# One transpose for the sample's values in the mLSTM layer, written into the keys' PSUM bank

## The chip, the cores and the metric

One core of a Trainium2 chip runs the whole step. Its engines work side by side: TensorE (PE) multiplies and transposes and writes to PSUM, VectorE (DVE) and ScalarE (ACT) read PSUM and do the elementwise work, GpSimd (POOL) does small masks and copies, SyncE (SP) issues the transfers. The metric is the device time of one execution in microseconds; each number is the median of several runs.

## What is computed

The reference is one step of a two-layer trunk over 256 prompt tokens and 64 sample tokens (8 sequences of 8 tokens), 320 in all. Layer 0 mixes with a spatial gate, layer 1 with an mLSTM matrix memory; a gated convolution network follows each. The change lies in layer 1. Cut to what matters there:

```python
p = x @ w_in
qk, new_buf = causal_dwconv(qk_pre, conv_buf, conv_w, conv_b)
k = qk[..., QK_B // 2:].reshape(bsz, s, H_B, DK_B) * (DK_B ** -0.5)
v32 = v.astype(jnp.float32).reshape(bsz, s, H_B, DV_B)
sc = jnp.einsum('bhtd,bhsd->bhts', qc, kc) * w_intra
num = w_inter[..., None] * jnp.einsum('bhtd,bhde->bhte', qc, C) \
    + jnp.einsum('bhts,bhse->bhte', sc, vc)
kg = kc * g[..., None]
C_new = decay[..., None, None] * C + jnp.einsum('bhsd,bhse->bhde', kg, vc)
```

There are 8 heads; keys have 128 elements a head, values 256. Products run in float32 split into a high part (fp32r) and a low part, with three products for one.

## The kernel before

Activations lie with features on the partitions and the 320 tokens on the free axis. Every projection is a row of blocks of 128 output features: `block` (with `chunk` and `take`) multiplies one 128-column slice of the weights by all tokens into one PSUM bank of the pool `psm` (three banks, tag `pm`). The pool `psa` (five banks, tag `pa`) holds the rest. `take` also runs the pipeline of the weights: `prefetch` issues the transfer four pieces ahead (line 127) and, one piece ahead, splits a landed piece into its high part `wh` on ACT (line 154) and its low part `wl` on DVE (line 155).

All PE instructions are pinned to the order in which the program writes them (`mm`, `tr`, `pin`; lines 54 and 57). The instructions of the other engines are ordered by a planner among those that are ready; `tc.issue_after(x)` adds that what its body writes on the engine of x is issued behind x.

Layer 1 (`layer_b`) loops over the heads `h`. One turn, in PE's order: the q block and its convolution (`qk_epi`), the k block, the state products and numerators of the head before (`inter`, `numer`), the first v block (`v_epi(h, 0)`), `state_prompt` and the first half of `state_sample` of the head before, the second v block (`v_epi(h, 1)`), `scores`, the two blocks of the output gate (`o_epi`) with more of `state_sample`, `finish` of the head before, then `k_nat(h)`, `v_nat(h)`, and the first state products `inter(h, 0)`. From head 4 on blocks of the output projection (`early`) come between.

- `v_epi` (line 786) copies a value block from PSUM to `vT` with ACT: 320 columns (line 788), and the 64 sample columns once more (line 789), so that the third group of 128 columns holds the sample's tokens twice.
- `k_nat` (line 863) transposes the keys in three groups of 128 tokens into columns 0 to 383 of one bank, `pk`. ACT and DVE then read it in pairs: twice a pair for the sample's gated keys `kgs` (lines 878 and 879), and one pair for each of the two prompt groups, `kgh` and `kgl` (lines 886 and 887).
- `v_nat` (line 841) transposes the values: three groups of tokens by two halves of 128 features, six transposes into two banks `pv`. ACT scales each group of 256 columns into `vh` (line 851), DVE takes the low part (line 854). For the sample the rows 0 to 63 of `vh[:, 2]` hold the high part and the rows 64 to 127 the low part; this is why its tokens are there twice. ACT copies them into `vb` (lines 856 and 857).
- `vh`, `vl` and `vb` are read by `numer` and the state updates of this head, which run in the next turn of the loop.
- `split` (line 311) keeps its two instructions in `self.parts`; after `qk_epi(h, 1)` `self.parts[1]` is the DVE instruction that makes `khl`, the low part of the keys that `scores` reads.

Of the kernel before, what the change touches and what calls it, by code (L numbers as in the profile page):

```python
# [10 lines left out]
F32 = mybir.dt.float32  # L11
F32R = mybir.dt.float32r
AF = mybir.ActivationFunctionType
ALU = mybir.AluOpType
MULT, ADD, SUB, MAX = ALU.mult, ALU.add, ALU.subtract, ALU.max

P = 128
EPS = 1e-6
TP = 256
NB, NS = 8, 8  # L20
T = TP + NB * NS
# [6 lines left out]
DV = 256  # L28
# [9 lines left out]
class Net:  # L38
# [597 lines left out]
    def layer_b(self):  # L636
        nc, tc, I, O = self.nc, self.tc, self.I, self.O
# [4 lines left out]
        with ExitStack() as ctx:  # L642
            lp = ctx.enter_context(tc.tile_pool(name="lb", bufs=1))
# [109 lines left out]
            S = [dict() for _ in range(NH)]  # L753
# [31 lines left out]

            def v_epi(h, j, ps):
                vT = lp.tile([P, 384], F32, tag="vT", name="vTb", bufs=2)
                nc.scalar.copy(vT[:, :T], ps[:, :T])
                nc.scalar.copy(vT[:, T:384], ps[:, TP:T])
                S[h].setdefault("vT", []).append(vT)  # L790

            def rows_in(h):
                mb = hp.tile([P, 392], F32, tag="Mb", name="Mb", bufs=2)
                nc.sync.dma_start(mb, I["rows"][h:h + 1, :].to_broadcast([P, 392]))
                S[h]["rows"] = mb
# [44 lines left out]

            def v_nat(h):
                s = S[h]
                pv = [self.psa.tile([P, 512], F32, tag="pa", name="pv") for _ in range(2)]
                dsts = [pv[t // 2][:, (t % 2) * DV:] for t in range(3)]
                for t in range(3):
                    for e in range(2):
                        self.tr(dsts[t][:, e * P:(e + 1) * P], s["vT"][e][:, t * P:(t + 1) * P], self.ident)
                for t in range(3):
                    dst = dsts[t]
                    sc = self.rc[:, t:t + 1]  # L850
                    nc.scalar.activation(vh[:, t, :DV], dst[:, :DV], AF.Copy, scale=sc)

                    r, out = (slice(0, P), vl[:, t, :DV]) if t < 2 else (slice(64, P), vh[64:, t, :DV])
                    nc.vector.scalar_tensor_tensor(out, dst[r, :DV], sc[r], vh[r, t, :DV].bitcast(F32), op0=MULT, op1=SUB)

                nc.scalar.copy(vb[:, :DV], vh[:, 2, :DV])
                nc.scalar.copy(vb[:32, :DV], vh[32:64, 2, :DV])
# [5 lines left out]
            def k_nat(h):  # L863
                s = S[h]
                ks = s["k"][0]
                pool, tag = (self.psm, "pm") if 0 < h < NH - 1 else (self.psa, "pa")
                pk = pool.tile([P, 512], F32, tag=tag, name="pk")
                for t in range(3):
                    self.tr(pk[:, t * P:(t + 1) * P], ks[:, t * P:(t + 1) * P], self.ident)
                kgh = hp.tile([P, 2, P], F32R, tag="kgh", name="kgh", bufs=1)  # L870
                kgl = hp.tile([P, 2, P], F32R, tag="kgl", name="kgl", bufs=1)
                kgs = hp.tile([P, 2, P], F32R, tag="kgs", name="kgs", bufs=1)
                kgz = hp.tile([P, NB, P], F32R, tag="kgz", name="kgz", bufs=1)
                g = colsT[:, 2, 32 + h:33 + h]
                src = pk[:, 2 * P:3 * P]

                for i, (r, o) in enumerate(((slice(0, 32), slice(32, 64)), (slice(32, 64), slice(0, 32)))):
                    nc.scalar.activation(kgs[:, i, :], src, AF.Copy, scale=g)
                    nc.vector.scalar_tensor_tensor(kgs[o, i, :], src[r], g[r], kgs[r, i, :].bitcast(F32), op0=MULT, op1=SUB)
                s["kg"] = (kgh, kgl, kgs, kgz)  # L880
                if h < NH - 1:
                    k_mask(h)
                for t in range(2):
                    g = colsT[:, t, 32 + h:33 + h]
                    src = pk[:, t * P:(t + 1) * P]
                    nc.scalar.activation(kgh[:, t, :], src, AF.Copy, scale=g)
                    nc.vector.scalar_tensor_tensor(kgl[:, t, :], src, g, kgh[:, t, :].bitcast(F32), op0=MULT, op1=SUB)

            def k_mask(h):
                _, _, kgs, kgz = S[h]["kg"]  # L890
                if h == NH - 1:
                    for b in range(NB):
                        nc.scalar.activation(kgz[:, b, :], kgs[:, b // 4, :].bitcast(F32), AF.Copy, scale=mk[:, b:b + 1])
                    return
                for i in (0, 4):
                    nc.gpsimd.tensor_tensor(kgz[:, i:i + 4, :], kgs[:, i // 4, :].bitcast(F32).unsqueeze(1).to_broadcast([P, 4, P]),
                                            mk[:, i:i + 4].unsqueeze(2).to_broadcast([P, 4, P]), op=MULT)
# [135 lines left out]
            def early(h, r):  # L1033
                for m in self.EARLY_OUT.get((h, r), ()):
                    self.residual(m, self.block(8, lambda k: Y[k]))
# [5 lines left out]
            vh = hp.tile([P, 3, CW], F32R, name="vh")  # L1041
            vl = hp.tile([P, 2, CW], F32R, name="vl")
# [18 lines left out]
            def blk():  # L1061
                return self.block(KD, self.x_rhs)
# [3 lines left out]
            def states(h, made):  # L1066

                state_in(h)
                with tc.issue_after(made.ins):
                    for i in (0, 1):  # L1070
                        state_split(h, i)
# [10 lines left out]
            for h in range(NH):  # L1082
                if h:
                    rows_in(h)
                    qk_epi(h, 0, blk())
                    early(h, 0)
                    if h == 1:
                        inter(0, 0)
                        state_split(0, 3)
                    inter(h - 1, 1)  # L1090
                    qk_epi(h, 1, blk())
                    for i in (2, 3):
                        inter(h - 1, i)
                    numer(h - 1)
                    early(h, 1)
                    ps = blk()
                    with self.behind_split():
                        stats(h - 1)
                    v_epi(h, 0, ps)
                    state_prompt(h - 1)  # L1100
                    made = state_sample(h - 1, 0)
                    early(h, 2)
                    v_epi(h, 1, blk())
                last = h == NH - 1
                if last:
                    with tc.issue_after(made.ins):
                        made = normed(h - 1)
                    states(h, made)
                if h:
                    made = state_sample(h - 1, 1)  # L1110
                    if not last:
                        with tc.issue_after(made.ins):
                            normed(h - 1)
                scores(h)
                early(h, 3)
                if h and not last:
                    o_epi(h, 0, blk())
                if last:
                    finish(h - 1)
                    begin(0)  # L1120
                if h:
                    for i in (2, 3) if last else (2,):
                        state_sample(h - 1, i)
                if last:
                    begin(1)

                    self.prefetch(0, self.used + 2)
                early(h, 4)
                if h and not last:
                    states(h, made)  # L1130
                if h and not last:
                    o_epi(h, 1, blk())
                if h and not last:
                    finish(h - 1)
                    state_sample(h - 1, 3)
                k_nat(h)
                v_nat(h)
                if h:
                    inter(h, 0)
                    for i in (2, 3):  # L1140
                        low = state_split(h, i)
                else:
                    with tc.issue_after(self.parts[0].ins), tc.issue_after(self.parts[1].ins):
                        state_split(0, 2)
                early(h, 5)
            nc.sync.dma_start(O["b_state"], nst)

            h = NH - 1
# [8 lines left out]
            ps = blk()  # L1157
# [14 lines left out]
            for m in range(KD):  # L1172
                ps = part.get(m)
                if ps is None:
                    ps = self.block(8, lambda k: Y[8 + k])
# [154 lines left out]
```

## Time and profile before

| what | value |
|---|---|
| median of 3 runs | 953.92 us (953.64 to 953.95) |
| the profiled execution | 954.62 us |
| its span, first to last instruction | 952.9 us |
| layer 1, heads 0 to 7 (from the first k transposes of head 0 to those of head 7) | 447.6 to 671.9 us |
| mean granted TensorE clock | 0.999 |
| HBM traffic | 163 GB/s over the span |

A line of the timeline gives the start in us, the time in us, the engine, the source line, the operation, the tile written and the tiles read, the shape, and how many were merged. A line of the groups ends in the count, then the busy us and the mean ns of one, then the idle us of the engine ahead of them with what ended it. A line of the waits gives the us in total, how often, and the longest. A line of the stretches gives the bounds and the length, the busy us of each engine with its instructions, the granted clock, the share of the DMA engines and their GB/s. The chain gives the start, the us and the work on it. Matmuls are pipelined: one lasts longer than the distance to the next, so lengths on PE are read from the chain.

### The profile page before, as it was taken

What the parts mean: (1) busy time and instruction counts of PE and PEld (TensorE: products, weight loads), DVE (VectorE), ACT (ScalarE), POOL (GpSimd) and SP (SyncE); (2) the same over time, 40 slices, a digit from 0 to 9 for tenths busy, and PEclk for the clock granted to TensorE, in tenths of its full rate; (3) what the DMA queues carried; (4) which work ended last, traced back from release to release, by engine and by line L of the source; (5) the groups of instructions that cost most, each with busy time, mean ns of one, the idle gap of its engine ahead of it and who ended that gap; (6) DMA issues with size and microseconds to landing.
All of it is one profiled execution on the core that took longest, in us unless ns stands there. A gap on an engine that the chain in (4) does not pass through costs nothing.

```text
span 952.9 us, 17084 instructions
## 1 busy us (share of the span) xinstructions
PE 945.6 (99%) x6420; PEld 932.8 (98%) x6420; DVE 695.6 (73%) x1324; ACT 530.5 (56%) x978; POOL 117.6 (12%) x291
## 2 busy tenths in 40 slices
PE   9999999999999999999999999999999999999997
PEld 8889999999999999999999999999999999999997
DVE  6766976577777764559999998788888777775443
ACT  7557543454554443348877767666765544554342
POOL 3200000010000000014442312303001000000000
PEclk9999999999999999999999999999999999999999
DMA  8643346544444455565465756654474444445541
GB/s 272 209 153 133 130 134 190 175 140 150 153 156 147 141 159 156 146 215 176 155 201 185 219 174 207 198 183 133 132 250 144 156 148 145 151 150 152 145 138 56
DMA packets 55238, 156.15 MB, mean 164 GB/s; under 512 B 7492, under 2 KB 13132, under 8 KB 55156
## 3 DMA queue, kind: packets, MB, share of 16 engines
q1 hardware_dynamic: 55156, 155.06, 51.2%
q8 instruction: 51, 0.84, 0.3%
q14 instruction: 31, 0.25, 0.1%
HBM read 143.05 MB, written 11.99 MB: 163 GB/s over the span
## 4 chain that ended last, share of the span: by engine, by line
PE 93%; DVE 3%; ACT 1%; issue 1%; POOL 0%; DMA 0%; SPq 0%; POOLq 0%; ACTq 0%
PE pm L54 80%; PE pv_a L54 6%; PE num L54 2%; PE pmix L54 1%; PE pcs L54 1%; PE pCp L54 1%; PE phn L57 0%; PE psc L54 0%; DVE wl L155 0%; PE pv L57 0%; PE pc L54 0%; ACT wh L154 0%; PE pg L54 0%; DVE Cl L911 0%; DMA raw<-in_a_wv 0%
## 5 line engine op out<-in xcount | busy, mean ns | idle before, releaser
L154 ACT CAST wh<-raw 128x1024 fp32r<-128x1024 f32 (+3 forms) x256 | 256.7, 1004 | 270.8 <-PE pm L54 141.5
L155 DVE TENSOR_TENSOR wl<-raw,wh 128x1024 fp32r<-128x1024 f32 (+3 forms) x256 | 298.8, 1168 | 121.0 <-ACT wh L154 116.5
L54 PE MATMUL pm<-xh,wh 128*128 128x320 f32 x1216 | 372.2, 311 | 0.0
L54 PE MATMUL pm<-xl,wh 128*128 128x320 f32 x1216 | 370.3, 309 | 0.0
L54 PE MATMUL pm<-xh,wl 128*128 128x320 f32 x1216 | 321.2, 309 | 0.0
L54 PEld LDWEIGHTS pm<-xl,wh 128*128 128x128 f32 x1216 | 228.4, 188 | 0.2
L54 PEld LDWEIGHTS pm<-xh,wh 128*128 128x128 f32 x1216 | 228.3, 188 | 0.2
L54 PEld LDWEIGHTS pm<-xh,wl 128*128 128x128 f32 x1216 | 214.5, 188 | 0.0
L54 PE MATMUL pm<-yh_f,wh 128*128 128x320 f32 x352 | 108.8, 309 | 0.0
L54 PE MATMUL pm<-yl_f,wh 128*128 128x320 f32 x352 | 108.8, 309 | 0.0
L54 PE MATMUL pm<-yh_f,wl 128*128 128x320 f32 x352 | 108.8, 309 | 0.0
L54 PEld LDWEIGHTS pm<-yh_f,wh 128*128 128x128 f32 x352 | 66.1, 188 | 0.0
L54 PEld LDWEIGHTS pm<-yl_f,wh 128*128 128x128 f32 x352 | 66.1, 188 | 0.0
L54 PEld LDWEIGHTS pm<-yh_f,wl 128*128 128x128 f32 x352 | 66.1, 188 | 0.0
L532 DVE SCALAR_TENSOR_TENSOR fcv<-fpad,vecs,fcv 128x336 f32<-128x336 f32 x88 | 49.5, 565 | 2.1 <-ACT fcv L530 0.6
L54 PE MATMUL pm<-yh_a,wh 128*128 128x320 f32 x128 | 39.6, 310 | 0.0
L54 PE MATMUL pm<-yh_a,wl 128*128 128x320 f32 x128 | 39.5, 309 | 0.0
L54 PE MATMUL pm<-yl_a,wh 128*128 128x320 f32 x128 | 39.5, 309 | 0.0
L534 ACT ACTIVATE fgl<-fcv 128x256 f32<-128x256 f32 x44 | 18.3, 415 | 37.9 <-DVE fcv L532 37.8
L54 PE MATMUL pm<-yhb,wh 128*128 128x320 f32 x128 | 38.2, 311 | 0.0
L54 PE MATMUL pm<-ylb,wh 128*128 128x320 f32 x128 | 37.9, 309 | 0.0
L304 DVE TENSOR_TENSOR xT<-pm,xT 128x320 f32<-128x320 f32 x39 | 19.0, 488 | 24.7 <-PE pm L54 24.5
(289 smaller groups left out, 1366.5 us busy)
## 6 DMA issues: line engine op xcount, KB each, us to landing
raw<-in_f_up SPq DMA_DIRECT2D x88, 512.0 KB, 3.3
raw<-in_b_win SPq DMA_DIRECT2D x48, 512.0 KB, 4.1
raw<-in_f_dn SPq DMA_DIRECT2D x32, 448.0 KB, 3.4
C<-in_C SPq DMA_DIRECT2D x32, 258.0 KB, 3.9
out_Cs<-C SPq DMA_DIRECT2D x32, 258.0 KB, 4.0
raw<-in_a_win SPq DMA_DIRECT2D x16, 512.0 KB, 3.2
raw<-in_a_wo SPq DMA_DIRECT2D x16, 512.0 KB, 4.0
raw<-in_f_dn SPq DMA_DIRECT2D x16, 512.0 KB, 3.6
```

The costliest lines, as they stand in the source:

```text
L54: self.pin(self.nc.tensor.matmul(out, lhsT, rhs, start=start, stop=stop, skip_group_check=skip))
L154: self.last_split = self.hold(nc.scalar.copy(wh[:, :kn, :], raw[:, :kn, :]))
L155: self.last_low = nc.vector.tensor_tensor(wl[:, :kn, :], raw[:, :kn, :], wh[:, :kn, :].bitcast(F32), op=SUB)
L304: self.nc.vector.tensor_tensor(x, ps[:, :T], x, op=ADD)
L532: nc.vector.scalar_tensor_tensor(cv, pd[:, i:i + NC], self.vec(w + i * KF), cv, op0=MULT, op1=ADD)
L534: nc.scalar.activation(gl[:, :TP], cv[:, :TP], AF.Gelu_apprx_tanh)
```

## The change

For the heads 1 to 7 the sample's 64 columns of both value blocks are copied side by side into one tile `vS` instead of twice behind each other in `vT`. One transpose of `vS` then gives both halves of the features, the first in the rows 0 to 63 and the second in the rows 64 to 127. It is written to columns 384 to 511 of the bank `pk`, the columns that the keys leave free, and `pv` is one bank instead of two. ACT and DVE take the high and the low part from there in two pairs of 64 rows by 128 columns. Head 0 stays as it was.

Besides, the second value block of heads 1 to 7 runs within `tc.issue_after(self.parts[1].ins)`: the DVE instructions that it issues, which is the low part of the next piece of weights (the output gate's first block, in the last head a piece of the output projection), are issued behind `khl`.

```diff
             def v_epi(h, j, ps):
                 vT = lp.tile([P, 384], F32, tag="vT", name="vTb", bufs=2)
-                nc.scalar.copy(vT[:, :T], ps[:, :T])
-                nc.scalar.copy(vT[:, T:384], ps[:, TP:T])
+                if h:
+                    nc.scalar.copy(vT[:, :TP], ps[:, :TP])
+
+                    if not j:
+                        S[h]["vS"] = lp.tile([P, P], F32, tag="vS", name="vS", bufs=1)
+                    nc.scalar.copy(S[h]["vS"][:, 64 * j:64 * j + 64], ps[:, TP:T])
+                else:
+                    nc.scalar.copy(vT[:, :T], ps[:, :T])
+                    nc.scalar.copy(vT[:, T:384], ps[:, TP:T])
...
             def v_nat(h):
                 s = S[h]
-                pv = [self.psa.tile([P, 512], F32, tag="pa", name="pv") for _ in range(2)]
-                dsts = [pv[t // 2][:, (t % 2) * DV:] for t in range(3)]
-                for t in range(3):
+                both = "vS" in s
+                pv = [self.psa.tile([P, 512], F32, tag="pa", name="pv") for _ in range(1 if both else 2)]
+                dsts = [pv[0][:, t * DV:(t + 1) * DV] for t in range(2)] + [s["pk"][:, 384:] if both else pv[1]]
+                for t in range(2 if both else 3):
                     for e in range(2):
                         self.tr(dsts[t][:, e * P:(e + 1) * P], s["vT"][e][:, t * P:(t + 1) * P], self.ident)
-                for t in range(3):
-                    dst = dsts[t]
+                if both:
+                    self.tr(dsts[2][:, :P], s["vS"], self.ident)
+                for t in range(2):
                     sc = self.rc[:, t:t + 1]
-                    nc.scalar.activation(vh[:, t, :DV], dst[:, :DV], AF.Copy, scale=sc)
-
-                    r, out = (slice(0, P), vl[:, t, :DV]) if t < 2 else (slice(64, P), vh[64:, t, :DV])
-                    nc.vector.scalar_tensor_tensor(out, dst[r, :DV], sc[r], vh[r, t, :DV].bitcast(F32), op0=MULT, op1=SUB)
+                    nc.scalar.activation(vh[:, t, :DV], dsts[t][:, :DV], AF.Copy, scale=sc)
+                    nc.vector.scalar_tensor_tensor(vl[:, t, :DV], dsts[t][:, :DV], sc, vh[:, t, :DV].bitcast(F32), op0=MULT, op1=SUB)
+
+                lo = slice(64, P)
+                if both:
+                    for e, r in enumerate((slice(0, 64), lo)):
+                        c, sc = slice(e * P, (e + 1) * P), self.rc[r, 2:3]
+                        nc.scalar.activation(vh[:64, 2, c], dsts[2][r, :P], AF.Copy, scale=sc)
+                        nc.vector.scalar_tensor_tensor(vh[lo, 2, c], dsts[2][r, :P], sc, vh[:64, 2, c].bitcast(F32), op0=MULT, op1=SUB)
+                else:
+                    sc = self.rc[:, 2:3]
+                    nc.scalar.activation(vh[:, 2, :DV], dsts[2][:, :DV], AF.Copy, scale=sc)
+                    nc.vector.scalar_tensor_tensor(vh[lo, 2, :DV], dsts[2][lo, :DV], sc[lo], vh[lo, 2, :DV].bitcast(F32), op0=MULT, op1=SUB)
...
                 for t in range(3):
                     self.tr(pk[:, t * P:(t + 1) * P], ks[:, t * P:(t + 1) * P], self.ident)
+                s["pk"] = pk
                 kgh = hp.tile([P, 2, P], F32R, tag="kgh", name="kgh", bufs=1)
...
                     early(h, 2)
-                    v_epi(h, 1, blk())
+
+                    with tc.issue_after(self.parts[1].ins):
+                        ps = blk()
+                    v_epi(h, 1, ps)
```

## The prediction

> **What bounds the kernel now.** I read the page first, then the waits of TensorE (PE), then the chain of waits and the timeline of one head.
>
> ```profile
> span 952.9 us, 17084 instructions
> ...
> PE 945.6 (99%) x6420; PEld 932.8 (98%) x6420; DVE 695.6 (73%) x1324; ACT 530.5 (56%) x978; POOL 117.6 (12%) x291
> ...
> PE 93%; DVE 3%; ACT 1%; issue 1%; POOL 0%; DMA 0%; SPq 0%; POOLq 0%; ACTq 0%
> ```
>
> PE is busy for 945.6 of 952.9 us, and 93% of the chain that ended last is PE. Busy time alone could hide waiting, so the waits of PE over the whole span come next; this is all of them.
>
> ```profile
> PE pw L54 <- PEq L1310: 0.8, 1, 0.8
> PE num L54 <- DVE y_b L1027: 0.3, 1, 0.3
> PE pv_a L54 <- DVE wh L146: 0.2, 1, 0.2
> ```
>
> In the memory layer PE waits once, for 0.3 us. So anything taken off PE's stream is a gain to the end, anything that VectorE (DVE) or ScalarE (ACT) does besides is free as long as PE finds its data, and **a new wait of PE is lost in full**: no slack of PE is there to take it up. The chain in time order prices the stretch that the change touches, here in head 2:
>
> ```profile
> 505.60 0.33 PE pk L57 x3
> 505.93 0.66 PE pv L57 x6
> 506.58 0.47 PE num L54 x4
> 507.06 3.52 PE pm L54 x24
> ```
>
> Three key transposes (pk), six value transposes (pv), the first part of the state products (num), and then the next head's q block (pm), without a gap.
>
> **The change, part by part.**
>
> *One transpose less.* Six transposes take 0.66 us on the chain, so one is 0.11 us. Heads 1 to 7 lose one each: 7 x 0.11 = 0.77 us off PE.
>
> *The engines around it.* Rows by form of the heads 1 to 6:
>
> ```profile
> L788 ACT COPY vTb<-pm 128x320 f32<-128x320 f32 x12 | 5.0, 413 | 0.7 <-PE pm L54 0.6
> ...
> L851 ACT ACTIVATE vh<-pv,rc 128x256 fp32r<-128x256 f32 x18 | 7.8, 470 | 0.9 <-DVE vl L854 0.2
> L854 DVE SCALAR_TENSOR_TENSOR vh<-pv,rc,vh 64x256 fp32r<-64x256 f32 x6 | 2.9, 491 | 0.2
> L886 ACT ACTIVATE kgh<-pk,cols 128x128 fp32r<-128x128 f32 x12 | 4.4, 368 | 0.0
> L887 DVE SCALAR_TENSOR_TENSOR kgl<-pk,cols,kgh 128x128 fp32r<-128x128 f32 x12 | 4.1, 341 | 0.0
> ```
>
> The copy of 320 columns (413 ns) shrinks to 256; two of them per head save between nothing and 0.08 us each (a fifth of the row). The sample's ACT scaling of 256 columns (470 ns) becomes two of 64x128; the nearest row, 128x128 from the same kind of bank, is 368 ns, so 0.74 us, 0.27 more. The DVE subtraction (491 ns) becomes two at 341 ns, 0.19 more. Together under 0.5 us a head on engines for which PE does not wait; what hides it is the q and k blocks of the next head (3.52 us each), which run before the products with vh. With that cover gone it would be 7 x 0.46 = 3.2 us. I cost it at nothing.
>
> *The low parts of the output gate's weights.* The added order is that this DVE instruction (wl) issues behind the low part of the keys (khl).
>
> ```profile
> 494.06 0.27 DVE L312 TENSOR_TENSOR khl<-qs,kh 128x128 fp32r<-128x128 f32 x1
> ...
> 496.80 1.22 DVE L155 TENSOR_TENSOR wl<-raw,wh 128x1024 fp32r<-128x1024 f32 x1
> ```
>
> The gate's low part (496.80 in head 2) already comes 2.5 us behind the end of khl. The edge only fixes what happens; should the order turn without it, a wl in front would delay the keys by its 1.2 us. Cost: nothing.
>
> *Where the new transpose writes.* This decides the sum. The transpose goes to columns 384 to 511 of pk, a bank whose columns 0 to 383 ACT and DVE read eight times in `k_nat` (two kgs pairs, the kgh/kgl pairs), and `k_nat` is written ahead of `v_nat`. Does an access to one bank wait for another engine's earlier access to other columns of it? The timeline of head 2 answers it for ACT and DVE:
>
> ```profile
> 505.76 0.82 PE L57 MATMUL pv<-ident,vTb 128*128 128x128 f32 x6
> ...
> 506.20 0.35 ACT L878 ACTIVATE kgs<-pk,cols 128x128 fp32r<-128x128 f32 x1
> ...
> 506.41 1.18 DVE L1030 SCALAR_TENSOR_TENSOR ylb<-y_b,gnh,yhb 128x320 fp32r<-128x320 f32 x2
> ...
> 507.62 0.62 ACT L910 CAST Ch<-C 128x516 fp32r<-128x516 f32 x1
> ...
> 508.02 0.34 DVE L879 SCALAR_TENSOR_TENSOR kgs<-pk,cols,kgs 32x128 fp32r<-32x128 f32 x1
> ...
> 508.39 0.37 ACT L878 ACTIVATE kgs<-pk,cols 128x128 fp32r<-128x128 f32 x1
> ...
> 508.90 0.34 DVE L879 SCALAR_TENSOR_TENSOR kgs<-pk,cols,kgs 32x128 fp32r<-32x128 f32 x1
> ...
> 509.28 0.37 ACT L886 ACTIVATE kgh<-pk,cols 128x128 fp32r<-128x128 f32 x1
> ...
> 509.28 0.49 DVE L854 SCALAR_TENSOR_TENSOR vh<-pv,rc,vh 64x256 fp32r<-64x256 f32 x1
> ...
> 510.20 0.34 DVE L887 SCALAR_TENSOR_TENSOR kgl<-pk,cols,kgh 128x128 fp32r<-128x128 f32 x1
> ...
> 510.58 0.37 ACT L886 ACTIVATE kgh<-pk,cols 128x128 fp32r<-128x128 f32 x1
> ...
> 511.06 0.42 DVE L762 TENSOR_TENSOR bpad<-pm,rb 128x256 f32<-128x256 f32 x1
> ...
> 511.40 0.34 DVE L887 SCALAR_TENSOR_TENSOR kgl<-pk,cols,kgh 128x128 fp32r<-128x128 f32 x1
> ```
>
> The eight readers strictly alternate ACT, DVE, ACT, DVE in program order, though ACT's second to fourth reading needs nothing that DVE makes: at 507.62 ACT takes a state cast from further down the program instead of the second kgs, which starts only when DVE's first reading has ended. In two heads ACT even sat idle for it; the view of that ACT line has, under the idle times before it, the releaser, the us and the times:
>
> ```profile
>   DVE kgs L879: 0.3, 2
> ```
>
> So one bank is shared in program order, whatever the columns. If that holds for ACT against DVE, I take it to hold for PE's write against both, and the new transpose, fifth of the value transposes, must wait for the second kgl. Queued behind it on PE are the state products and the next head's q block, that is everything.
>
> The Trainium skill speaks against this change too: "PSUM — Partial Sum Buffer", section "PSUM bank collisions raise a hardware error", says that two engines on one bank and 32-partition quadrant collide even at disjoint columns, and that software must keep them apart by bank. By it PE has to be held back; the trace has no PE write behind a reader of the same bank, so only the ACT/DVE half of the rule is seen here.
>
> *The length of the wait.* PE's fifth value transpose would start at 505.76 + 4 x 0.11 = 506.20; the second kgl ends at 511.40 + 0.34 = 511.74: 5.5 us. The first and the last of the seven heads:
>
> ```profile
> 476.92 0.82 PE L57 MATMUL pv<-ident,vTb 128*128 128x128 f32 x6
> ...
> 483.89 0.34 DVE L887 SCALAR_TENSOR_TENSOR kgl<-pk,cols,kgh 128x128 fp32r<-128x128 f32 x1
> ...
> 672.09 0.82 PE L57 MATMUL pv<-ident,vTb 128*128 128x128 f32 x6
> ...
> 676.04 1.22 DVE L155 TENSOR_TENSOR wl<-raw,wh 128x1024 fp32r<-128x1024 f32 x1
> 677.17 0.34 DVE L887 SCALAR_TENSOR_TENSOR kgl<-pk,cols,kgh 128x128 fp32r<-128x128 f32 x1
> ```
>
> 477.36 to 484.23 is 6.9 us, 672.53 to 677.51 is 5.0; heads 3 to 6 look like head 2. Sum: 6.9 + 5 x 5.5 + 5.0 = 39 us. Upper end: add a low part of 1.2 us in front of the last kgl (as at 676.04) in the six other heads, 46. Lower end, the eight readings back to back: 4 x 0.36 + 4 x 0.34 = 2.8 us from 506.20, seven times 20. In between: the sample's subtraction at 509.28 now comes after the wait and bpad at 511.06 needs PE, so 0.9 us leave the stretch, while a low part may fill it. I take 37 us, near the order that is seen, since ylb (506.41) stays in front.
>
> *The clock after a wait.* The trace shows one long idle time of PE, at the end, and a cold start:
>
> ```profile
> 5.29 0.57 PE L54 MATMUL pv_a<-wl,xh 128*128 128x256 f32 x2
> ...
> 6.42 0.40 PE L54 MATMUL pv_a<-wl,xh 128*128 128x256 f32 x2
> ...
> 947.00:948.00 1.00, 0.01 (x1) 0.00 (x0) 0.80 (x2) 0.77 (x2) 0.00 (x0) 1.00 0.39 129
> ...
> 951.00:952.90 1.90, 0.00 (x0) 0.00 (x0) 0.00 (x0) 0.00 (x0) 0.00 (x0) 0.54 0.21 80
> ```
>
> The granted clock (third figure from the end) averages 0.54 over the last 1.9 us, so it went to half at about 951.15, 4.1 us after PE's last work; and at the start PE works some 5 us (from 0.8 to 5.8) before a pair of the same products falls from 0.57 to 0.40 us. A stall of over 4 us can therefore cost up to 5 us at half speed, 2.5 us. Between 0 and 7 x 2.5 = 17.5 us; the stalls are a little longer than that idle time, and I take a third, 6 us.
>
> "TensorE: Matmul & The Clock Gate" in the Trainium skill ("What's actually happening") lets the clock fall after one idle window of about 3.4 us that runs freely; by that roughly half of stalls of 5.3 us would meet it, about 9 us by the 2.5 above, and the trace's 4.1 us agrees with it.
>
> **Sum.** Span 952.9 + 37 + 6 - 0.8 = 995.1, with the 1.7 us around the span (954.62 profiled) 996.8; the profiled execution lies 0.7 above the median of 953.92, so **996 us**, 4.4% slower.
>
> **The rivals.** (1) *No wait, not slower.* Only overlapping columns order PE against the readers. Then 953.92 - 0.77 = 953.1, and with the 0.3 us wait gone 952.8. For it: write and reads share no column, and no PE write behind a reader is seen. Against it: ACT's readings share no column with DVE's later ones either, and wait. It decides if PE's fifth value transpose starts within about 0.1 us of the fourth. (2) *A short wait.* The planner draws the eight readings together, 20 us in all and no clock loss: 953.1 + 20 = 973. Against it: ylb, C and the split of the next weights are ready earlier and go first now. (3) *The clock falls at every stall*: 953.1 + 37 + 17.5 = 1008. For it: 4.1 us are below most stalls; against it: an idle time shorter by a microsecond may just miss it.
>
> **How the numbers follow.** The forecast 59%, no wait 14%, short wait 12%, clock each time 15%. A measurement of this kernel tells about 0.2%, 1.9 us, from no change. No wait gives -0.8 to -1.1 us, mostly inside that: same 12%, faster 2%; the other cases are slower, 86%. The range 970 to 1013 takes in the short wait and the clock, with the longest order of readings up to 46, and leaves out the case without a wait.
>
> **What would show it.** Right: in heads 1 to 7 PE idle ahead of a pv/pk transpose, released by DVE kgl, 4 to 6 us each; PE's idle time over 35 us; a granted clock below 1 in those stretches. Wrong: no such wait and some 953 us. If the wait is there but 2 to 3 us long, the readings were drawn together; if it is there and the clock stays at 1.00, the term of 6 us falls.

## The result and the profile after

The changed kernel takes 1005.9 us (median of four runs, 1003.51 to 1007.52), beside 953.93 us before: 1.054 times as long, 95% interval 1.052 to 1.056. The profiled execution took 1004.64 us with a span of 1001.8, so 48.9 us of span were added. The page after, its head, the clock in slices and the chain by engine:

```profile
span 1001.8 us, 17107 instructions
...
PE 957.5 (96%) x6413; PEld 943.1 (94%) x6413; DVE 701.6 (70%) x1331; ACT 533.4 (53%) x985; POOL 113.5 (11%) x291
...
PEclk9999999999999999999889889998999999999999
...
PE 91%; DVE 5%; ACT 2%; issue 1%; DMA 0%; POOL 0%; SPq 0%; POOLq 0%; ACTq 0%
```

PE has seven instructions fewer (6413 for 6420) and yet is busy 12 us longer, since some of its work runs slower: the clock row dips to 8 in the middle. And PE is no longer busy throughout. All the waits of PE, in total us, times and the longest:

```profile
PE pk L57 <- DVE kgl L906: 37.9, 7, 7.1
PE pw L54 <- PEq L1332: 0.8, 1, 0.8
PE pv_a L54 <- ACT wh L154: 0.2, 1, 0.2
```

Seven waits, one per changed head, all of the new transpose for the last reading of the keys' bank: 37.9 us. The releaser is an instruction of DVE, so this is an order between instructions; what the chip would do without that order, no run shows. The wait of 0.3 us for y_b that the memory layer had before is gone. The first and the last of the seven in the timeline of PE, with the idle time and its releaser in brackets; the five between are 5.5 us each:

```profile
484.69 0.47 PE L57 MATMUL pk<-ident,vS 128*128 128x128 f32 x1 [7.11 <-DVE kgl L906]
...
722.53 0.33 PE L57 MATMUL pk<-ident,vS 128*128 128x128 f32 x1 [3.37 <-DVE kgl L906]
```

The chain of waits shows what PE waits for, here in head 2 (start, us, work), which before ran from pk to pm without a gap:

```profile
515.51 0.55 DVE ylb L1049
516.07 0.40 DVE C L1026
...
516.86 0.48 DVE vl L861
517.38 0.34 DVE kgs L898
517.75 1.37 DVE wl L155
519.15 0.36 DVE kgl L906
519.54 0.38 ACT kgh L905
519.94 0.36 DVE kgl L906
520.35 0.47 PE pk L57
520.82 0.86 PE num L54 x4
521.68 5.56 PE pm L54 x24
527.24 0.47 PE num L54 x4
527.71 3.52 PE pm L54 x24
```

The eight readings of the bank still go one behind the other, with a split of the next weights' low part (wl, 1.37 us) between them, and only then does PE transpose. Behind the wait the first block of 24 products takes 5.56 us; the second takes 3.52 as always. That is the clock. The stretches in which the granted clock was 0.50 (bounds, length, busy us by engine, clock, DMA share, GB/s), and as the last row the wait of head 7:

```profile
481.70:488.50 6.80, 3.81 (x16) 3.81 (x17) 4.22 (x8) 3.02 (x8) 2.66 (x2) 0.50 0.65 196
519.30:526.00 6.70, 5.66 (x22) 5.66 (x23) 2.34 (x6) 3.17 (x9) 1.82 (x5) 0.50 0.53 140
553.40:560.20 6.80, 3.36 (x14) 3.37 (x15) 3.82 (x8) 3.50 (x10) 4.08 (x6) 0.50 0.72 223
590.90:597.70 6.80, 5.42 (x22) 5.42 (x23) 2.65 (x7) 3.34 (x9) 2.12 (x5) 0.50 0.51 146
638.70:642.10 3.40, 2.89 (x12) 2.90 (x13) 1.45 (x4) 2.24 (x7) 1.24 (x5) 0.50 0.79 240
683.10:689.90 6.80, 4.89 (x20) 4.90 (x21) 3.17 (x7) 3.34 (x9) 2.64 (x5) 0.50 0.50 98
718.50:722.60 4.10, 0.73 (x7) 0.49 (x6) 2.82 (x8) 4.06 (x14) 0.00 (x0) 1.00 0.52 161
```

Six of the seven waits cost the clock. PE worked 3.81 + 5.66 + 3.36 + 5.42 + 2.89 + 4.89 = 26.0 us within those stretches, and half of it, 13.0 us, would not have been needed at the full clock. The bill of the span: 37.9 of waits, less 0.8 for the transposes, less the 0.3 us wait that is gone, leaves 48.9 - 36.8 = 12.1 us for the clock, close to those 13. How much the clock takes differs between executions: the four ran at mean granted clocks of 0.982, 0.981, 0.975 and 0.976 and took 1003.51, 1004.64, 1007.16 and 1007.52 us, so the bill is that of one of the two milder ones.

### The profile page after: what moved, and what is told of

It reads as the page before. It is cut to its first block, busy times and chain, and to the rows that moved or that the text cites. A ratio compares the mean times of both kernels' runs of the same rounds, so it can differ in the third digit from the quotient of the medians.

```text
span 1001.8 us, 17107 instructions
## 1 busy us (share of the span) xinstructions
PE 957.5 (96%) x6413; PEld 943.1 (94%) x6413; DVE 701.6 (70%) x1331; ACT 533.4 (53%) x985; POOL 113.5 (11%) x291
## 4 chain that ended last, share of the span: by engine, by line
PE 91%; DVE 5%; ACT 2%; issue 1%; DMA 0%; POOL 0%; SPq 0%; POOLq 0%; ACTq 0%
PE pm L54 78%; PE pv_a L54 6%; PE num L54 3%; DVE wl L155 1%; PE pmix L54 1%; PE pcs L54 1%; PE pCp L54 1%; ACT yhb L1048 1%; PE psc L54 1%; DVE kgl L906 1%; DVE kgs L898 0%; DMA raw<-in_a_wv 0%; DVE vl L861 0%; PE pk L57 0%; PE pc L54 0%
## 5 line engine op out<-in xcount | busy, mean ns | idle before, releaser
L54 PEld LDWEIGHTS pm<-xh,wh 128*128 128x128 f32 x1216 | 231.1, 190 | 0.2
L54 PEld LDWEIGHTS pm<-xl,wh 128*128 128x128 f32 x1216 | 230.9, 190 | 0.2
L54 PE MATMUL pm<-yhb,wh 128*128 128x320 f32 x128 | 41.4, 334 | 0.0
L54 PE MATMUL pm<-ylb,wh 128*128 128x320 f32 x128 | 41.0, 331 | 0.0
L57 PE MATMUL pk<-ident,vS 128*128 128x128 f32 x7 | 3.2, 454 | 37.9 <-DVE kgl L906 37.9
```

Source lines behind the costliest of these rows:

```text
L54: self.pin(self.nc.tensor.matmul(out, lhsT, rhs, start=start, stop=stop, skip_group_check=skip))
L57: self.pin(self.nc.tensor.transpose(out, in_, ident))
```

## The experiments

The theory after the result: the loss is the order of the new transpose behind the eight readings of its bank, plus the clock that follows the waits. The rivals: the new tile and pairs are late, the issue order holds something back, or the bank itself is dear to share.

**A bank of its own, and the order of issue by itself.** Three kernels. The first is the change with a second value bank:

```diff
-                pv = [self.psa.tile([P, 512], F32, tag="pa", name="pv") for _ in range(1 if both else 2)]
-                dsts = [pv[0][:, t * DV:(t + 1) * DV] for t in range(2)] + [s["pk"][:, 384:] if both else pv[1]]
+                pv = [self.psa.tile([P, 512], F32, tag="pa", name="pv") for _ in range(2)]
+                dsts = [pv[0][:, t * DV:(t + 1) * DV] for t in range(2)] + [pv[1]]
```

> The change with one thing undone: the single transpose of the sample's values goes to a second pv bank of its own instead of the keys' bank. If PE waits because the write comes behind eight readings of the same bank, the wait of PE for kgl is gone and the time is the one before less seven transposes, 953.9 - 0.8 = 953.1 us (952 to 954). If the new tile vS, the two pairs of 64 rows or the added issue order were what is late, PE still waits and the time stays above 990 us.

The second is the change without the issue order; the third is the kernel before with this diff turned round, the order alone.

```diff
-                    with tc.issue_after(self.parts[1].ins):
-                        ps = blk()
-                    v_epi(h, 1, ps)
+                    v_epi(h, 1, blk())
```

> The change without its second part: the issue order of the gate's low parts behind the keys' low part is taken out. If that order costs nothing, 1006 us (1002 to 1009) with the same seven waits for kgl. If it is what holds PE or DVE back, or what keeps a 1.2 us low part out of the keys' way, the time differs by some 8 us (7 x 1.2) in either direction.

> The kernel before with the second part alone. The order is already the one of the trace before, so 953.9 us (953.3 to 954.5), no difference. If the added order holds back the low part behind khl where PE needs it, some us more.

Own bank: 956.98 us, 1.0031 of before (1.0020 to 1.0041). Its waits of PE:

```profile
PE num L54 <- DVE y_b L1046: 1.1, 2, 0.6
PE pw L54 <- PEq L1332: 0.8, 1, 0.8
PE pcs L54 <- issue: 0.6, 1, 0.6
```

No wait for kgl: with the transpose, the tile vS, the pairs and the issue order all in place, taking the write out of the keys' bank removes 49 of the 52 us. The bank that the write goes to is the cause. (Each PSUM tile here has a bank to itself, so no run separates "the same bank" from "the same tile". In heads 1 to 6 `pk` is one of the three banks of `psm`, which the projections share; that these lack a bank is not the loss, since the list after the change has no wait of a `pm`.) But 953.1 was a miss: the time is 3 us above before, not 0.8 below. Without the issue order the change takes 1005.51 us (1003.61 to 1006.45) with 37.6 us of waits for kgl, the same as with it; and the order alone gives 1.0003 of before (0.9995 to 1.0012). So the second part of the change explains nothing of the loss.

**The transpose ahead of the readings.** Same bank, same columns, another place in the program:

```diff
                 s["pk"] = pk
+                if "vS" in s:
+                    self.tr(pk[:, 384:], s["vS"], self.ident)
...
-                if both:
-                    self.tr(dsts[2][:, :P], s["vS"], self.ident)
```

> The change with the single transpose moved: it goes to the same columns of the keys' bank, but stands directly behind the three key transposes, ahead of the eight readings. If only the order behind the readings costs, 953.1 us (952 to 954) and no wait of PE for kgl. If sharing the bank itself is dear (the pairs of the sample now run behind eight readings of the keys), PE waits elsewhere or the time stays some us above 954.

965.53 us, 1.0122 of before (1.0108 to 1.0136). No wait for kgl, as the theory had it, but the rival is right as well: PE waits elsewhere. The row of its waits, and the end of the longest but one of them, in head 2, from the last reading of the keys on:

```profile
PE num L54 <- DVE vh L866: 9.1, 4, 3.6
```

```profile
513.64 0.34 DVE L906 SCALAR_TENSOR_TENSOR kgl<-pk,cols,kgh 128x128 fp32r<-128x128 f32 x1
...
516.29 0.80 ACT L818 ACTIVATE w<-Mb,cols 128x256 f32<-128x256 f32 x2 [3.26 <-DMA Mb<-rows]
517.00 0.35 ACT L865 ACTIVATE vh<-pk,rc 64x128 fp32r<-64x128 f32 x1
...
517.38 0.34 DVE L866 SCALAR_TENSOR_TENSOR vh<-pk,rc,vh 64x128 fp32r<-64x128 f32 x1 [1.81 <-ACT vh L865]
...
518.05 1.03 ACT L154 CAST wh<-raw 128x1024 fp32r<-128x1024 f32 x1
...
519.11 0.36 ACT L865 ACTIVATE vh<-pk,rc 64x128 fp32r<-64x128 f32 x1
519.50 0.36 DVE L866 SCALAR_TENSOR_TENSOR vh<-pk,rc,vh 64x128 fp32r<-64x128 f32 x1
...
519.92 0.39 PE L54 MATMUL num<-vh,Ps 128*128 128x258 f32 x1 [3.24 <-DVE vh L866]
```

The sample's two pairs now come behind the eight readings of the keys in the same bank, and the numerator product, due some 10 us behind the transposes, finds vh unfinished. The queue in the bank is not the whole of this delay: the readings end at 513.98, but ACT stands idle until 516.29 for another instruction, whose input Mb a transfer brings, takes the first pair at 517.00, and then slips a weight split of 1.03 us between the two. With the pairs at the same place in the program and a bank of their own, no wait for vh is left. So a shared bank has two prices in these kernels: the writer waits for earlier readers, and later readers wait for earlier readers and then for whatever their engine has taken up meanwhile. Of the 11.6 us, 9.1 are these waits; the longest, 3.6 us in head 7, also cost the clock for 3.4 us.

**The pairs ahead of the readings, and the own bank without the order.** To see whether anything is left of the 0.8 us, the transpose stays in the keys' bank behind the key transposes, and the two pairs are written ahead of `kgs` in `k_nat`:

```diff
+                if "vS" in s:
+                    self.tr(pk[:, 384:], s["vS"], self.ident)
+                    lo = slice(64, P)
+                    for e, r in enumerate((slice(0, 64), lo)):
+                        c, sc = slice(e * P, (e + 1) * P), self.rc[r, 2:3]
+                        nc.scalar.activation(vh[:64, 2, c], pk[r, 384:], AF.Copy, scale=sc)
+                        nc.vector.scalar_tensor_tensor(vh[lo, 2, c], pk[r, 384:], sc, vh[:64, 2, c].bitcast(F32), op0=MULT, op1=SUB)
                 kgh = hp.tile([P, 2, P], F32R, tag="kgh", name="kgh", bufs=1)
```

> The transpose behind the three key transposes in the keys' bank, and the sample's two pairs ahead of the eight readings of the keys, with the added issue order. If the 9.1 us of waits for vh, with the transpose first, come from the pairs queueing behind those readings, they are gone: 953 to 955 us. If the later keys then make PE wait for kgl, kgh or kgz, some us more.

> The same without the added issue order. If the order is what brings small waits into the kernels that have it, 953.1 us, 1 to 3 us below the one with it; if it does nothing, the same time.

> The single transpose in a bank of its own, without the added issue order. If the 0.3% by which the own bank with the order is slower than before comes from the order (a low part in front of the output gate's product and so of y_b, for which PE waits twice), 953.1 us (952.5 to 954). If it comes from the new pairs and the copies into vS, 957 us again.

| kernel | us | ratio to before, 95% | PE's waits in the memory layer |
|---|---|---|---|
| own bank, with the order | 956.98 | 1.0031 (1.0020 to 1.0041) | y_b 1.1, issue 0.6 |
| own bank, without it | 954.78 | 1.0008 (0.9999 to 1.0017) | y_b 1.1 |
| pairs first, with the order | 957.62 | 1.0038 (1.0025 to 1.0051) | vh 2.7, xT 0.8, wh 0.5 |
| pairs first, without it | 955.76 | 1.0013 (1.0004 to 1.0022) | bns 1.0, xT 0.7 |

With the pairs first the 9.1 us of waits for vh are 2.7 us for vh at another product, or none. The order costs about 2 us in both pairs of kernels; which instruction pays is not settled, since the spans of the two own-bank profiles (954.1 and 953.9) hardly differ: the one with the order is of the fastest of its seven executions, 955.78 us. None of the three reaches the 953 us that was expected, and no version is faster than before. The row of the own bank without the order says where the 0.8 us can have gone:

```profile
PE num L54 <- DVE y_b L1046: 1.1, 3, 0.4
```

The state products behind the transposes wait three times for y_b, 1.1 us, where it was once and 0.3 before. That the earlier arrival of PE only lengthens this wait is one reading of the rows and not shown. Against it stands the kernel with the order alone: it has all its transposes, its time is that of before, and its trace shows 0.9 us of waits for y_b. Where the 0.8 us went stays open.

**The clock.** PE is given work during its waits, into a bank that nobody reads:

```diff
                 if both:
+                    fill = self.psa.tile([P, 512], F32, tag="pa", name="fill")
+                    for i in range({1: 44, NH - 1: 19}.get(h, 34)):
+                        self.mm(fill[:, :T], self.xh[:, 0, :P], self.xh[:, 0, :], True, True)
                     self.tr(dsts[2][:, :P], s["vS"], self.ident)
```

> The change with PE kept at work during its waits: 44, 34 and 19 products of 128x320 into a bank that nobody reads stand ahead of the single transpose in head 1, in heads 2 to 6 and in head 7 (233 in all, 0.147 us each). If what the change costs beyond its 37.9 us of waits is the clock, the clock stays at 0.999 and the time is 953.9 + 37.9 - 0.8 = 991 us (986 to 995). If the rest has another cause, the time stays at 1003 us or more.

993.94 us, 1.0415 of before (1.0399 to 1.0430). The wait row and the stretch of head 1 that before the filling ran partly at 0.50:

```profile
PE pk L57 <- DVE kgl L909: 4.4, 7, 1.2
```

```profile
481.00:489.00 8.00, 7.33 (x52) 7.07 (x51) 5.13 (x10) 4.30 (x10) 3.02 (x2) 1.00 0.63 193
```

233 products of 0.147 us (an estimate: 3.52 us for 24) are 34.2 us, and 4.4 of waits remain: 38.6 in place of 37.9. The clock is 1.00 in this stretch and 0.999 in the whole, and the time is 12.0 us below the change's 1005.9, with 233 products more. So the rest beyond the waits is the clock, but for some 2 us: 953.9 + 38.6 - 0.8 would be 991.7. That the reading of the bank ends no earlier when PE works shows too that PE's idling is not what delays it.

**Shorter waits.** Two kernels. In one the transpose, the pairs and the copies of vb, gathered in `v_tail`, follow the next head's q block:

```diff
-                    qk_epi(h, 0, blk())
+                    ps = blk()
+                    if h > 1:
+                        v_tail(h - 1)
+                    qk_epi(h, 0, ps)
...
             begin(0)
+            v_tail(h)
```

In the other the low part of the next weights is issued behind the second kgl:

```diff
-                    nc.vector.scalar_tensor_tensor(kgl[:, t, :], src, g, kgh[:, t, :].bitcast(F32), op0=MULT, op1=SUB)
+                    s["kgl"] = nc.vector.scalar_tensor_tensor(kgl[:, t, :], src, g, kgh[:, t, :].bitcast(F32), op0=MULT, op1=SUB)
...
-                    qk_epi(h, 0, blk())
+                    with tc.issue_after(S[h - 1]["kgl"].ins):
+                        ps = blk()
+                    qk_epi(h, 0, ps)
...
-                early(h, 5)
+                with tc.issue_after(S[h]["kgl"].ins):
+                    early(h, 5)
```

> The change with the single transpose, its two pairs and the copies of vb moved behind the next head's q block (in head 7 behind the first 12 products of the output projection). If the end of the eight readings sets the wait, 4.0 us of PE's work (the 0.48 us of state products and the 3.52 us of the block) now run under it: 7.1 becomes 3, 5.5 becomes 1.5 in heads 2 and 3, nothing is left in heads 4 to 6, which have further blocks between, and head 7 keeps 1: about 7 us in all, 960 us (956 to 966), and no wait is long enough for the clock. If the readings start late because PE is late, the waits stay near 5 us and the time above 975 us.

> The change with one more order: the low part of the weights that DVE takes between the readings in heads 1 to 6 (1.2 to 1.4 us in front of kgl) is issued behind the second kgl. If it lengthens the wait, each of the six waits shrinks by 1.0 to 1.4 us, 31 us in all, and some of them are then too short for the clock: 985 to 998 us. If the readings end when they do for another reason, 1006 us as for the change.

Later: 970.02 us, 1.0168 of before (1.0151 to 1.0185). Heads 4 to 6 wait no more, as expected; the other four wait 3.5, 2.1, 2.0 and 4.1 us, 11.7 in all where 7 were expected, and the wait of 4.1 us drops the clock once. It is head 7's, where 1 us was expected, for two reasons. Six products, not 12, stand ahead of the transpose there. And two low parts of 1.2 us (at 682.68 and 684.08) now stand ahead of the last two readings, where the changed kernel has none. The direction is the theory's, the 960 us a miss.

Keys first: 1001.0 us, 4.9 below the change, where 985 to 998 were expected. Its waits of PE, and rows of its stretches:

```profile
PE pk L57 <- DVE kgl L906: 31.2, 7, 4.6
PE pm L54 <- DVE wl L155: 2.4, 1, 2.4
```

```profile
455.50:458.90 3.40, 1.23 (x8) 1.23 (x9) 3.40 (x6) 3.35 (x8) 2.59 (x5) 1.00 0.06 16
458.90:462.20 3.30, 3.30 (x17) 3.30 (x16) 3.04 (x6) 2.17 (x5) 2.92 (x5) 0.50 0.86 286
...
482.80:489.50 6.70, 4.12 (x17) 4.12 (x18) 5.64 (x10) 3.61 (x9) 2.04 (x2) 0.50 0.52 154
520.40:523.60 3.20, 3.20 (x14) 3.20 (x14) 1.55 (x3) 1.37 (x4) 0.54 (x2) 0.50 0.65 185
```

The waits of heads 1 to 6 shrank to 4.63 us each, so the low part between the readings did lengthen them by 0.9 us (2.5 in head 1, where two low parts are gone). The edge also held back a low part behind head 0's kgl, in the first q block, for 2.4 us. But the clock fell at all seven waits and once more after those 2.4 us: the time fell by about what all the waits lost (37.9 less 33.6), and the clock gave back nothing. In head 2 the half clock starts as PE resumes, so all 3.2 us of it are work.

## Why the prediction held, and where it was off

The forecast was 996 us, 4.4% slower; 1005.9 us is 5.4% slower and in the range. Of the 9.9 us between them, 6.7 lie in the profiled span (1001.8 for 995.1), and 6 of these are the clock's. The rest is no step of the mechanism: the profiled execution lies 1.3 us below its median instead of 0.7 above, and 2.8 us instead of 1.7 stand around the span.

- *PE is the bound, a new wait is lost in full.* Right: 37.9 us of waits stand in a span that grew by 48.9, and the filled kernel shows the rest to be the clock's.
- *The bank decides.* Right, and taken from ACT against DVE readings alone: PE's write waits for the last reading of other columns, in every changed head; in a bank of its own there is no such wait. The step from reading against reading to write against reading was an assumption, and it held.
- *The length of the waits, 37 us.* 37.9, and that it is so near is in part luck. In heads 2 to 6 the 5.5 us of the order seen before came true with other contents: bpad and the sample's subtraction left the stretch, and a low part of 1.2 to 1.4 us filled it, as at the upper end of the estimate. The last head is shorter (3.4 for 5.0): no low part stands in front of its last reading.
- *The clock, 6 us.* The term that was mis-sized: 12 us. I took a third of the most that all seven could lose, 17.5 us, with no row of the trace for the third. Six of seven lost the clock, and 2.2 us each on average (13.0 / 6). The rival in which every stall loses it, 1008 us at 15%, was nearer than the forecast.
- *The rule of the clock.* The step "by that roughly half of stalls of 5.3 us would meet it", from the Trainium skill, "TensorE: Matmul & The Clock Gate", section "What's actually happening", was too mild too. All six waits of 5.5 us and more, and those of 4.6 us, lost it; the rows of the kernel with the keys first show a loss behind a window of 3.4 us in which PE was busy 1.23 us, so it need not be an idle one.
- *One transpose less, 0.8 us.* PE has the seven transposes less, but in no version does the time show them; the cause stays open.
- *The engines around it, at nothing.* In the changed kernel right, and the durations were near (rows of the groups of heads 1 to 6, change):

```profile
L867 ACT ACTIVATE vh<-pk,rc 64x128 fp32r<-64x128 f32 x12 | 4.3, 357 | 1.1 <-PE pk L57 1.0
L868 DVE SCALAR_TENSOR_TENSOR vh<-pk,rc,vh 64x128 fp32r<-64x128 f32 x12 | 4.2, 351 | 13.8 <-ACT vh L867 13.6
```

  357 for 368 ns and 351 for 341. But the price of the cover being gone, 3.2 us, counted only their own time. With the transpose first the pairs cost 9.1 us, since they stand behind the other readings of the bank and what ACT takes up after these.
- *The issue order, at nothing.* Right for the change and for the order alone; in the kernels with the transpose and without the stalls it costs about 2 us.
- *No wait, 953.1 us.* Refuted as a rival, and as a goal: the kernels without the wait end at 954.8 to 957.6 us.

## What to carry to other kernels

Free columns of a PSUM bank were not free in any of these kernels: whoever writes or reads there takes a place in the line of all accesses to that bank, in program order, so a write belongs ahead of the bank's readings and its own readers first among them. Where PE is the bound, price a stall by its length and then by the clock behind it: here every stall of 3.6 us and more cost the clock, in the changed kernel 2.2 us each on average, and of those of 2 to 3.5 us some did (2.4 and 3.4 us) and others did not (2.0, 2.1, 3.2, 3.4 and 3.5 us), by a rule that the next section reads from the traces. And 0.8 us of instructions taken off the bounding engine showed in no measured time here, so such a gain is not to be counted before it is measured.

## What was not expected of the hardware

The half clock comes and goes in whole steps of 3.41 us: by the clock's own record in the traces each stretch at 0.50 in this layer lasts 3.41 or 6.83 us (the bounds of the rows above are rounded), and the starts of the six (481.7, 519.3, 553.4, 590.9, 638.7, 683.1) lie 37.6, 34.1, 37.5, 47.8 and 44.4 us apart, which is 11, 10, 11, 14 and 13 times 3.41. So the same wait loses the clock or keeps it by where it falls: 3.4 us in head 7 kept it in the changed kernel and lost it in the kernel with the keys first and in the one without the order, and a wait of 2.4 us lost it there too, with the keys first.

Laid on these steps, the traces show what decides. Six windows of 3.41 us: two of the changed kernel, one without the order and one with the keys first, all at full clock, then one with the keys first and one without the order, at half clock. The first figure behind the length is PE's busy time, with the ends that the profile models.

```profile
549.97:553.38 3.41, 1.39 (x13) 1.15 (x11) 3.26 (x8) 2.03 (x5) 0.00 (x0) 1.00 0.77 282
720.64:724.05 3.41, 1.52 (x11) 1.53 (x12) 1.58 (x5) 3.38 (x12) 0.00 (x0) 1.00 0.25 54
717.68:721.09 3.41, 1.28 (x11) 1.04 (x9) 2.91 (x9) 3.37 (x9) 0.00 (x0) 1.00 0.59 178
629.54:632.95 3.41, 1.50 (x14) 1.26 (x12) 3.29 (x8) 2.03 (x5) 0.00 (x0) 1.00 0.14 38
588.58:591.99 3.41, 2.66 (x11) 2.67 (x12) 1.53 (x3) 1.15 (x4) 0.49 (x2) 0.50 0.50 152
519.71:523.12 3.41, 2.90 (x12) 2.90 (x13) 1.10 (x4) 2.23 (x7) 1.28 (x5) 0.50 0.83 246
```

Behind the first and the third window (1.39 and 1.28 us of work) the clock is half, behind the second and the fourth (1.52 and 1.50 us) it stays full. Behind the fifth (2.66 us) the half clock goes on, behind the sixth (2.90 us) it ends. In the twelve traces of this case that holds without exception: all 35 windows at full clock with at most 1.40 us of PE work are followed by half, and none of the others, which have 1.50 us or more; a window at half clock keeps it with at most 2.66 us of work and ends it with 2.90 or more. So a window loses the clock with some 2 us or more of idle time in it. An estimate from this: a stall under 2 us by itself does not cost the clock, one over 4 us does, since one of the windows that it touches gets 2 us of it, and between them the place decides.

And the block of the same shape takes 5.56 us for 24 products right behind a stall, where 3.52 is the rule, so a slow block in a chain can be the echo of a wait that lies before it.
